# Buffers, ScalarE's order, gather pacing and one-hot layout in the expert phase of a hybrid decoder block

## The chip, the cores and the metric

The kernel runs on one core of one Trainium2 chip. The metric is the device time of one execution in microseconds (us), taken as the median of three runs. Inputs are drawn from a fixed seed, and the program is the same in every run.

## The reference, cut to what matters

A decoder layer on 512 tokens plus 16 meta tokens (width 2048): attention and an mLSTM in parallel, then a PEER layer over 16,384 experts (`u` and `v`, each 16,384 x 2048 in float32). The change touches the PEER layer alone:

```
q = (ht @ w_q)                                  # 8 heads x 2 halves x 128
s = einsum('thpd,hpnd->thpn', q, sub_keys)      # scores against 2 x 128 sub-keys
s1, i1 = top_k(s[..., 0, :], 16);  s2, i2 = top_k(s[..., 1, :], 16)
best_s, best_pos = top_k(s1[:, :, None] + s2[:, None, :], 16)
idx  = (i1 * 128 + i2) at best_pos              # 128 experts for each token
gate = softmax(best_s)
act  = gelu(einsum('td,tkd->tk', h, u[idx]))
y    = einsum('tk,tkd->td', gate * act, v[idx])
```

## The kernel before, in words

The 512 tokens are split. For 352 of them (`ND`) the kernel computes every expert densely: U multiplies them with all of `u` in 128 chunks of 128 experts, applies gelu, and stores the result in a scratch array `Ad`; a gate table `Gd`, zero except where an expert was chosen, is built beside it; V multiplies `Ad` times `Gd` with all of `v`. For the other 160 tokens the chosen rows of `u` and `v` are gathered from memory, one row for each token (128 rows of 8 KB) in one indirect DMA that GpSimd issues. There are 320 such gather steps (`NJ`): 160 with `u`, then 160 with `v`. VectorE takes each: a multiply with an accumulated sum for `u` (L844), a scaled addition for `v` (L855, L857). Three row buffers `ug` rotate.

**Chunks.** A float32 weight is split into a high and a low part, both in TensorE's faster float32 form, and each product takes three matmuls (L89 to L91): 48 for a chunk of U. `load_half` (L70) loads half a chunk, 512 KB, into a buffer `raw` by SyncE's DMA queue; `split_half` (L75) makes `hi` on ScalarE (L79, tiles `hid`, in V `hiv`) and `lo` on VectorE (L80, `lod`, `lov`). Three `raw` and five `hi` and `lo` buffers rotate; the number in a tile's name is the step, 16 more than the chunk of U. `u_chunk` (L886) runs `step`: split the next chunk, 48 matmuls into a PSUM tile `pu`, then gelu on ScalarE into `at` (L889) and its DMA to `Ad` on ScalarE's queue (L890).

**Gate table.** From chunk 33 on, each chunk of U is followed by one group of `gbuild` (five times two) until chunk 115, 88 groups in all. A group covers four tokens. `ebuild` makes, ahead of it, the one-hot rows of the two index halves for these tokens (`e`, two VectorE operations, L1076 and L1077), the second times the three bfloat16 parts of the gate (`ea` on ScalarE, L1081; `eg` on VectorE, L1079). These tiles hold the four tokens interleaved: `[128, 128, 4]`, so that one token's 128 values lie 8 bytes apart, but for `ea`, which is contiguous. `gbuild` runs 12 matmuls 128 x 128 x 128 in bfloat16 (L1092: for each token one with `ea` and two with `eg` as the moving side, `e` always as the weights) into `pg`, and ScalarE copies the group into `stg` (L1093). There is one `stg` buffer; eight groups fill it, and then SyncE's queue writes its 2 MB to `Gd` (L1095).

**Pacing.** `run(n)` takes gather steps until n are done and prefetches three. In U, `pace(c)` spreads them evenly from chunk 33 to the last one so that `JU` = 150 are done at the end of U; V takes the rest, evenly. The last six chunks of U (`UTAIL`) are also where the first eight tiles of V's moving side are prepared: `p_load` (DMAs of `gt` from `Gd`, `av` from `Ad`, on ScalarE's queue), `p_mul` (`tm`, VectorE), `p_split` (`ah` on ScalarE, `al` on VectorE). V then takes 240 half chunks of `v` through eight PSUM banks (`tmm`, L1275 to L1277: 24 matmuls each) and 16 more in another form.

**Order.** PE's program order is written by hand throughout (`manual_schedule`), VectorE's from the routing on, GpSimd's from the gate table on. ScalarE's and SyncE's orders come from a scheduler, which places an instruction by when it expects its inputs.

Of the kernel before, what the change touches and what calls it, by code (L numbers as in the profile page):

```python
# [43 lines left out]
ND = S - 128 - NB  # L44
GROUPS = [8] + [16] * 7 + [8]
NJ = 2 * (128 + SB)
JU = 150
AR = 20
AR1 = 8

# [1 line left out]
def bcast(ap, n):  # L52
    return bass.AP(tensor=ap.tensor, offset=ap.offset, ap=[list(a) for a in ap.ap] + [[0, n]])


def bcast_mid(ap, n):
    a = [list(p) for p in ap.ap]
    return bass.AP(tensor=ap.tensor, offset=ap.offset, ap=a[:1] + [[0, n]] + a[1:])


def body(tc, I, out):
    nc = tc.nc
    top = ExitStack()
    with top:
# [3 lines left out]
        dp = top.enter_context(tc.tile_pool(name="dp", bufs=1, space=DRAM))  # L68

        def load_half(src, name, rawp=None):  # L70
            raw = (rawp or wp).tile([128, 8, 128], F, name="raw" + name, tag="raw", bufs=3)
            nc.sync.dma_start(raw, src.rearrange("p (k c) -> p k c", k=8))
            return raw

        def split_half(src, name, raw=None, eng=nc.vector):  # L75
            raw = raw or load_half(src, name)
# [6 lines left out]
        def split_tile(src, name):  # L83
            return [split_half(src[b], f"{name}_{b}") for b in range(2)]

        def mm3(ps, w, k, xh, xl, cs):
            hi, lo = w[k // 8]
# [578 lines left out]
def rest(tc, I, out, L):  # L666
# [150 lines left out]
    up = sU.enter_context(tc.tile_pool(name="up", bufs=1))  # L817
    iota = up.tile([128, 128], F, name="iota")
    nc.scalar.dma_start(iota, I["c_iota"])
    iota4 = up.tile([128, 128, 4], BF, name="iota4")  # L820
    nc.vector.tensor_copy(iota4, bcast(iota, 4))
    n1T = up.tile([128, ND], BF, name="n1T")
    n2T = up.tile([128, ND], BF, name="n2T")
    gp = up.tile([128, 3, ND], BF, name="gp")
# [46 lines left out]
    sp = [I["wq"][i] for i in range(16)] + [I["u"][c] for c in range(NK)]  # L871
    w[2] = split_tile(sp[2], "d2")

    def step(n, mid=None):
        if n + 1 < len(sp):
            w[n + 1] = split_tile(sp[n + 1], f"d{n + 1}")
        ps = pmu.tile([128, 512], F, name="pu", tag="pu")
        nn = S if n < 16 else ND
        for k in range(KD):
            mm3(ps[:, :nn], w[n], k, h2h, h2l, slice(0, nn))  # L880
            if k == 7 and mid:
                mid()
# [180 lines left out]

    with tc.tile_pool(name="gk", bufs=1, reuse_waits="tile") as gk, \
            tc.tile_pool(name="psg", bufs=2, space=PSUM) as psg, \
            tc.manual_schedule(engines={mybir.EngineType.Pool}):
        stg = {}

        ge = {}

        def ebuild(q):
            t0 = 4 * q
            e = gk.tile([128, 2, 128, 4], BF, name="e", tag="e", bufs=2)
            eg = gk.tile([128, 2, 128, 4], BF, name="eg", tag="eg", bufs=2)
            ea = gk.tile([128, 4, 128], BF, name="ea", tag="ea", bufs=2)
            nc.vector.tensor_tensor(e[:, 0], iota4, bcast_mid(n1T[:, t0:t0 + 4], 128), op=OP.is_equal)  # L1076
            nc.vector.tensor_tensor(e[:, 1], iota4, bcast_mid(n2T[:, t0:t0 + 4], 128), op=OP.is_equal)  # L1077
            for i in range(2):
                nc.vector.tensor_tensor(eg[:, i], e[:, 1], bcast_mid(gp[:, 1 + i, t0:t0 + 4], 128), op=OP.mult)  # L1079
            for j in range(4):  # L1080
                nc.scalar.activation(ea[:, j, :], e[:, 1, :, j], AF.Copy, scale=g0[:, t0 + j:t0 + j + 1])  # L1081
            ge[q] = e[:, 0], [ea.rearrange("p j n -> p n j"), eg[:, 0], eg[:, 1]]

        def gbuild(q):
            tg, r = divmod(4 * q, TG)
            if r == 0:
                stg[tg] = gk.tile([128, NK, TG], F, name="stg", tag="stg")
            e1, eg = ge.pop(q)
            pg = psg.tile([128, 4, 128], F, name="pg", tag="pg")
            for j in range(4):  # L1090
                for i in range(3):
                    nc.tensor.matmul(pg[:, j, :], e1[:, :, j], eg[i][:, :, j], start=(i == 0), stop=(i == 2))  # L1092
            nc.scalar.copy(stg[tg][:, :, r:r + 4], pg.rearrange("p j n -> p n j"))  # L1093
            if r + 4 == TG:
                nc.sync.dma_start(Gd[tg, :, 0:NK, :], stg[tg])  # L1095

        gr2.append(sG.enter_context(tc.tile_pool(name="gr2", bufs=1, side="right")))
        acc["D"] = gr2[0].tile([128, D], F, name="h2nB", tag="h2nB")
        for q in range(NQ):
            nc.scalar.dma_start(acc["D"][NB * q:NB * q + NB], hB)  # L1100
        ng, n0, c0 = 0, nj[1], ci
        ebuild(0)

        def pace(c):
            run(n0 + int((c + 1 - c0) * (JU - n0) / (NK - c0)))

        for c in range(ci, NK - UTAIL):
            u_chunk(c)
            while ng < min(ND // 4, (c + 1 - ci) * (ND // 4) / (NK - 12 - ci)):
                gbuild(ng)  # L1110
                ng += 1
                if ng < ND // 4:
                    ebuild(ng)
            pace(c)
    sU.close()

    with ExitStack() as sV:
        vp = sV.enter_context(tc.tile_pool(name="vp", bufs=1, side="right", reuse_waits="tile"))
        pool_order = sV.enter_context(tc.manual_schedule(engines={mybir.EngineType.Pool}))
        g0s = [sum(GROUPS[:g]) for g in range(len(GROUPS) + 1)]  # L1120
        gts, ats, tms, A = {}, {}, {}, {}

# [35 lines left out]
        def vload(i):  # L1158
            if i < len(vord):
                g, dc, pr, c = vord[i]  # L1160
                vraw[i] = load_half(I["v"][g0s[g] // 2 + pr, dc if g == NG - 1 else 2 * dc + c], "v",
                                    None if i % 6 < 3 and i < nlast - 4 else vr[0])

        def vsplit(i):
            if i < len(vord):
# [27 lines left out]
        for c in range(NK - UTAIL, NK):  # L1193
            if c == NK - 1:
                for i in range(VLA):
                    vload(i)
                    vsplit(i)
            u_chunk(c)
            for _ in range(-(-len(pro) // (NK - c))):
                f, q = pro.pop(0)  # L1200
                f(q)
            pace(c)
        assert not pro
        sQ.close()
        sD.close()
# [258 lines left out]
```

## Time and profile before

| | |
|---|---|
| Median of three runs | 3330.11 us (3321.87 to 3330.35) |
| Profiled execution | 3331.74 us, its span 3330.0 us, mean granted clock 0.992 |
| TensorE busy | 98% of the span (20,126 matmuls) |
| VectorE, ScalarE, GpSimd busy | 70%, 40%, 28% |
| Moved by DMA | 815.47 MB, 245 GB/s over the span |

The profile follows one execution. Busy shares of TensorE count overlapping matmuls, so that the engine can be called busy while it runs slower than it could; the number of matmuls in a stretch tells more. "Idle before" is the time that an engine stood still before an instruction, with what ended it.

### The profile page before, as it was taken

How to read it: one execution, taken by the hardware profiler on the slowest of the kernel's cores; microseconds unless marked ns; L12 is line 12 of the kernel's file. 1: busy time of each engine (PE TensorE's matmuls, PEld its weight loads, DVE VectorE, ACT ScalarE, POOL GpSimd, SP SyncE). 2: the span in 40 equal slices, each digit the busy share in tenths (PEclk: the TensorE clock that was granted, in tenths of full speed). 3: DMA queues.
4: the chain of work that ended last, by engine and by line, in shares of the span. 5: the costliest groups of instructions: out<-in, count | busy, mean ns of one | idle time of the engine just before them, and what ended most of it. 6: DMA issues, size and time to landing. Idle time of an engine off the chain costs nothing.

```text
span 3330.0 us, 51020 instructions
## 1 busy us (share of the span) xinstructions
PE 3264.0 (98%) x20126; PEld 3067.1 (92%) x20126; DVE 2320.2 (70%) x3504; ACT 1325.5 (40%) x2219; POOL 943.9 (28%) x942
## 2 busy tenths in 40 slices
PE   8999999999999999999999999997999999999998
PEld 7889898888887899999999999997999999999996
DVE  7444444444367788787877778767888888888973
ACT  5444444453252233444544544433333333333323
POOL 2011111110015566423332233322323323323312
PEclk8999999999999999999999999998999999999999
DMA  4222121123353266588888978999999999999972
GB/s 154 70 70 77 64 77 64 64 70 115 127 186 136 87 221 226 206 323 316 332 343 325 361 297 348 354 362 337 377 354 375 372 365 370 375 364 372 379 279 101
DMA packets 230162, 815.47 MB, mean 245 GB/s; under 512 B 21697, under 2 KB 85697, under 8 KB 186529
## 3 DMA queue, kind: packets, MB, share of 16 engines
q1 hardware_dynamic: 105488, 400.72, 33.3%
q0 software_dynamic: 46080, 335.56, 25.7%
q10 hardware_dynamic: 78352, 75.92, 6.8%
q8 instruction: 158, 2.59, 0.3%
q14 instruction: 84, 0.68, 0.1%
HBM read 757.33 MB, written 54.79 MB: 244 GB/s over the span
## 4 chain that ended last, share of the span: by engine, by line
PE 85%; DVE 8%; DMA 2%; issue 2%; ACT 1%; POOL 1%; ACTq 0%; SPq 0%; POOLq 0%; DVEq 0%
PE pu L89 10%; PE pu L90 10%; PE pu L91 10%; PE py L1275 8%; PE py L1277 8%; PE py L1276 8%; PE ps L89 5%; PE ps L91 5%; PE ps L90 5%; PE pg L1092 3%; PE po L742 2%; PE po L740 2%; PE po L741 2%; DVE y L857 1%; DVE lov L80 1%
## 5 line engine op out<-in xcount | busy, mean ns | idle before, releaser
L89 PE MATMUL pu<-hh,hid 128*128 128x352 f32 (+1 forms) x2272 | 759.8, 334 | 0.2 <-ACT at L889 0.2
L90 PE MATMUL pu<-hh,lod 128*128 128x352 f32 (+1 forms) x2272 | 751.3, 331 | 3.1 <-DVE lod L80 3.1
L91 PE MATMUL pu<-hl,hid 128*128 128x352 f32 (+1 forms) x2272 | 750.2, 330 | 0.0
L1275 PE MATMUL py<-ah,hiv 128*128 128x352 f32 x1920 | 627.0, 327 | 20.5 <-ACT hiv L79 9.5
L1276 PE MATMUL py<-ah,lov 128*128 128x352 f32 x1920 | 623.4, 325 | 8.8 <-DVE lov L80 8.8
L1277 PE MATMUL py<-al,hiv 128*128 128x352 f32 x1920 | 625.5, 326 | 0.0
L79 ACT CAST hiv<-rawv 128x1024 fp32r<-128x1024 f32 x256 | 269.2, 1053 | 572.4 <-PE py L1277 462.6
L80 DVE TENSOR_TENSOR lod<-rawd,hid 128x1024 fp32r<-128x1024 f32 x284 | 361.0, 1287 | 176.7 <-ACT hid L79 175.5
L90 PEld LDWEIGHTS pu<-hh,lod 128*128 128x128 f32 x2272 | 428.2, 188 | 12.8 <-DVE lod L80 3.4
L89 PEld LDWEIGHTS pu<-hh,hid 128*128 128x128 f32 x2272 | 429.9, 189 | 10.3 <-ACT at L889 0.8
L91 PEld LDWEIGHTS pu<-hl,hid 128*128 128x128 f32 x2272 | 428.1, 188 | 9.7
L79 ACT CAST hid<-rawd 128x1024 fp32r<-128x1024 f32 x284 | 297.8, 1050 | 347.2 <-DMA rawd<-in_u_dram 235.1
L89 PE MATMUL ps<-xh,hiz 128*128 128x256 f32 (+2 forms) x1280 | 410.9, 321 | 1.3 <-DVE qT L369 1.2
L836 POOL DMA_INDIRECT ug<-in_un_dram,idx x128 | 249.2, 1947 | 522.3 <-DVE ug L844 500.8
L91 PE MATMUL ps<-xl,hiz 128*128 128x256 f32 (+2 forms) x1280 | 392.8, 307 | 0.0
L90 PE MATMUL ps<-xh,loz 128*128 128x256 f32 (+2 forms) x1280 | 392.5, 307 | 0.0
L1275 PEld LDWEIGHTS py<-ah,hiv 128*128 128x128 f32 x1920 | 363.0, 189 | 24.2 <-issue 12.9
L1276 PEld LDWEIGHTS py<-ah,lov 128*128 128x128 f32 x1920 | 362.6, 189 | 11.8 <-DVE lov L80 11.8
L836 POOL DMA_INDIRECT ug<-in_vn_dram,idx x128 | 229.0, 1789 | 469.7 <-DVE y L857 444.3
L1277 PEld LDWEIGHTS py<-al,hiv 128*128 128x128 f32 x1920 | 361.9, 188 | 0.0
L80 DVE TENSOR_TENSOR lov<-rawv,hiv 128x1024 fp32r<-128x1024 f32 x256 | 313.4, 1237 | 33.7 <-ACT hiv L79 33.5
L857 DVE SCALAR_TENSOR_TENSOR y<-ug,act,y 128x2048 f32<-128x2048 f32 x127 | 298.3, 2349 | 14.8 <-DMA ug<-in_vn_dram,idx 14.8
(342 smaller groups left out, 5029.9 us busy)
## 6 DMA issues: line engine op xcount, KB each, us to landing
rawd<-in_u_dram SPq DMA_DIRECT2D x256, 512.0 KB
rawv<-in_v_dram SPq DMA_DIRECT2D x256, 512.0 KB
rawz<-in_wz_dram SPq DMA_DIRECT2D x98, 512.0 KB
Ad<-at ACTq DMA_DIRECT2D x128, 176.0 KB
Gd<-stg SPq DMA_DIRECT2D x11, 2048.0 KB
gt<-Gd ACTq DMA_DIRECT2D x32, 704.0 KB
av<-Ad ACTq DMA_DIRECT2D x64, 352.0 KB
rawwo<-in_wo_dram SPq DMA_DIRECT2D x40, 512.0 KB
```

Of the source, the lines that this page charges most:

```text
L79: nc.scalar.copy(hi, raw)
L80: eng.tensor_tensor(lo, raw, hi.bitcast(F), op=OP.subtract)
L89: nc.tensor.matmul(ps, a, xh[k][:, cs], start=(k == 0), stop=False)
L90: nc.tensor.matmul(ps, b, xh[k][:, cs], start=False, stop=False)
L91: nc.tensor.matmul(ps, a, xl[k][:, cs], start=False, stop=(k == KD - 1))
L740: nc.tensor.matmul(ps[tb], mh[n][:, sl], h, start=(n == 0), stop=False)
L836: nc.gpsimd.indirect_dma_start(out=t, out_offset=None, in_=I["un" if kind in "dD" else "vn"], in_offset=bass.IndirectOffsetOnAxis(ap=ix[:, ...
L857: nc.vector.scalar_tensor_tensor(acc[kind], t, o, acc[kind], op0=OP.mult, op1=OP.add)
L1092: nc.tensor.matmul(pg[:, j, :], e1[:, :, j], eg[i][:, :, j], start=(i == 0), stop=(i == 2))
L1275: nc.tensor.matmul(po, h, ah, start=(pr + j == 0), stop=False)
L1276: nc.tensor.matmul(po, l, ah, start=False, stop=False)
L1277: nc.tensor.matmul(po, h, al, start=False, stop=(2 * pr + j == n - 1))
```

## The change

Five `raw` buffers stand in U from the gate table on: the three of before and two in a pool of their own, taken in turn. The split of a chunk is issued two chunks ahead, right behind the store of `at`, where it was one chunk ahead. ScalarE's order is written by hand from the gate table on (through the rest of U, and V). `JU` is 166, and the gather steps are paced to end at chunk 121, so that the last six chunks hold none; V is left with 154 where it had 170. The one-hot tiles hold two tokens interleaved, twice (`[128, 2, 128, 2]`), so that a token's values lie 4 bytes apart.

```diff
-JU = 150
+JU = 166
-            raw = (rawp or wp).tile([128, 8, 128], F, name="raw" + name, tag="raw", bufs=3)
+            pool, n = rawp or (wp, 3)
+            raw = pool.tile([128, 8, 128], F, name="raw" + name, tag="raw", bufs=n)
...
-    iota4 = up.tile([128, 128, 4], BF, name="iota4")
-    nc.vector.tensor_copy(iota4, bcast(iota, 4))
+    iota2 = up.tile([128, 2, 128, 2], BF, name="iota2")
+    for i in range(2):
+        nc.vector.tensor_copy(iota2[:, i], bcast(iota, 2))
...
+    ru = []
+
+    def uload(n):
+        if n < len(sp) and n not in w:
+            ps = [None, None]
+            if ru:
+                for b in range(2):
+                    if ru[1] % 5 in (1, 3):
+                        ps[b] = (ru[0], 2)
+                    ru[1] += 1
+            w[n] = split_tile(sp[n], f"d{n}", ps)
+
     def step(n, mid=None):
-        if n + 1 < len(sp):
-            w[n + 1] = split_tile(sp[n + 1], f"d{n + 1}")
+        uload(n + 1)
...
         nc.scalar.dma_start(Ad[c // 4, :, c % 4, :], at)
+        if ru:
+            uload(c + 18)
...
-            tc.manual_schedule(engines={mybir.EngineType.Pool}):
+            tc.manual_schedule(engines={mybir.EngineType.Pool, mybir.EngineType.Activation}), \
+            tc.tile_pool(name="ru", bufs=1, reuse_waits="tile") as rup:
         stg = {}
+        ru += [rup, 0]
+
+        def pairs(t):
+            a = [list(p) for p in t.ap]
+            return bass.AP(tensor=t.tensor, offset=t.offset, ap=[a[0], [2 * a[1][0], 2], [0, 128], [a[1][0], 2]])
...
-            nc.vector.tensor_tensor(e[:, 0], iota4, bcast_mid(n1T[:, t0:t0 + 4], 128), op=OP.is_equal)
+            nc.vector.tensor_tensor(e[:, 0], iota2, pairs(n1T[:, t0:t0 + 4]), op=OP.is_equal)
...
-                    nc.tensor.matmul(pg[:, j, :], e1[:, :, j], eg[i][:, :, j], start=(i == 0), stop=(i == 2))
+                    nc.tensor.matmul(pg[:, j, :], e1[:, j // 2, :, j % 2], eg[i][:, j // 2, :, j % 2],
+                                     start=(i == 0), stop=(i == 2))
...
-            run(n0 + int((c + 1 - c0) * (JU - n0) / (NK - c0)))
+            run(n0 + int((c + 1 - c0) * (JU - n0) / (NK - UTAIL - c0)))
...
+        ru.clear()
...
-        pool_order = sV.enter_context(tc.manual_schedule(engines={mybir.EngineType.Pool}))
+        pool_order = sV.enter_context(tc.manual_schedule(engines={mybir.EngineType.Pool, mybir.EngineType.Activation}))
...
                 f(q)
-            pace(c)
```

PE's order is the same instruction for instruction. ScalarE's around chunk 79 of U (step 95), where a new `stg` begins, stood so before:

```order
L1081 ACTIVATE ea_18178<-e_18176,g0_9082 128x128 x4
L79 CAST hid95_1_18198<-rawd95_1_18196 128x1024
L889 ACTIVATE at_18158<-pu_18109 128x352
L890 DMA Ad_9071<-at_18158 128x352
L1081 ACTIVATE ea_18270<-e_18268,g0_9082 128x128 x4
L1093 COPY stg_18161<-pg_18162 128x128x4
L79 CAST hid96_0_18287<-rawd96_0_18285 128x1024
L79 CAST hid96_1_18293<-rawd96_1_18291 128x1024
```

And so it stands now, at the same place:

```order
L1116 COPY stg_17527<-pg_18117 128x128x4
L1102 ACTIVATE ea_18134<-e_18132,g0_9083 128x128 x4
L902 ACTIVATE at_18198<-pu_18149 128x352
L903 DMA Ad_9071<-at_18198 128x352
L80 CAST hid95_0_18203<-rawd95_0_18201 128x1024
L80 CAST hid95_1_18209<-rawd95_1_18207 128x1024
L1116 COPY stg_18213<-pg_18214 128x128x4
L1102 ACTIVATE ea_18230<-e_18228,g0_9083 128x128 x4
```

Where a new `stg` begins (`stg_18161`, now `stg_18213`), its first copy stood behind the `ea` of the next group; now it stands ahead of it. Both halves of `hid` for a step stand together, behind `at` and its store.

VectorE's order around step 141 (chunk 125, one of the last six) stood so before (`ug` with `actB` is a gather step):

```order
L844 SCALAR_TENSOR_TENSOR ug_22097,actB_9063<-ug_22097,h2nB_13800 128x2048
L844 SCALAR_TENSOR_TENSOR ug_22164,actB_9063<-ug_22164,h2nB_13800 128x2048
L80 TENSOR_TENSOR lod141_0_22339<-rawd141_0_22336,hid141_0_22338 128x1024
L80 TENSOR_TENSOR lod141_1_22345<-rawd141_1_22342,hid141_1_22344 128x1024
L1146 TENSOR_TENSOR al_22401<-tm_22328,ah_22400 128x352
L1135 TENSOR_TENSOR tm_22404<-av_22243,gt_22239 128x352
L1146 TENSOR_TENSOR al_22407<-tm_22404,ah_22406 128x352
L844 SCALAR_TENSOR_TENSOR ug_22248,actB_9063<-ug_22248,h2nB_13800 128x2048
```

Now the same stretch of VectorE reads:

```order
L1170 TENSOR_TENSOR al_22402<-tm_22399,ah_22401 128x352
L1159 TENSOR_TENSOR tm_22409<-av_22327,gt_22323 128x352
L81 TENSOR_TENSOR lod141_0_22414<-rawd141_0_22411,hid141_0_22413 128x1024
L81 TENSOR_TENSOR lod141_1_22420<-rawd141_1_22417,hid141_1_22419 128x1024
L1170 TENSOR_TENSOR al_22476<-tm_22409,ah_22475 128x352
L1159 TENSOR_TENSOR tm_22479<-av_22327,gt_22323 128x352
L1170 TENSOR_TENSOR al_22482<-tm_22479,ah_22481 128x352
L81 TENSOR_TENSOR lod142_0_22490<-rawd142_0_22487,hid142_0_22489 128x1024
```

The gather steps are gone from it; the splits and the preparation of V's first tiles stay.

## Rows read from the trace of the kernel before

**Rows 1.** The page: busy us of each engine; shares of the last chain.

```profile
PE 3264.0 (98%) x20126; PEld 3067.1 (92%) x20126; DVE 2320.2 (70%) x3504; ACT 1325.5 (40%) x2219; POOL 943.9 (28%) x942
PE 85%; DVE 8%; DMA 2%; issue 2%; ACT 1%; POOL 1%; ACTq 0%; SPq 0%; POOLq 0%; DVEq 0%
```

**Rows 2.** Stretches: U with gate groups, its end, V's start, V.

```profile
core 0: us, PE busy (x) PEld busy (x) DVE busy (x) ACT busy (x) POOL busy (x), PEclk, DMA share, GB/s
1411.00:2164.00 753.00, 752.43 (x5099) 740.25 (x5098) 591.28 (x762) 368.02 (x701) 235.12 (x118) 1.00 0.87 332
2164.00:2264.00 100.00, 94.74 (x578) 93.63 (x576) 64.34 (x69) 31.82 (x44) 28.15 (x15) 0.98 0.94 357
2264.00:2380.00 116.00, 99.93 (x564) 96.65 (x565) 84.39 (x96) 42.10 (x67) 32.22 (x19) 0.93 0.94 351
2380.00:3190.00 810.00, 798.72 (x4914) 795.58 (x4914) 710.21 (x655) 259.45 (x303) 265.05 (x148) 1.00 0.97 368
```

**Rows 3.** Tile pg, 1440 to 2160: matmul durations in ns, min/median/max.

```profile
L1092 PE MATMUL pg<-eg,e x671: 273/294/303, 1439.7 to 2155.0; 128*128 128x128 bf16 x168
L1092 PE MATMUL pg<-ea,e x335: 237/238/249, 1439.9 to 2154.8; 128*128 128x128 bf16 x168
```

**Rows 4.** Timeline of PE around one gate group: start us, us, what.

```profile
1707.13 0.32 PE L90 MATMUL pu<-hh,lod 128*128 128x352 f32 x1
1707.29 0.32 PE L91 MATMUL pu<-hl,hid 128*128 128x352 f32 x1
...
1708.81 0.32 PE L90 MATMUL pu<-hh,lod 128*128 128x352 f32 x1
```

**Rows 5.** VectorE by group, 1440 to 2160: busy us, mean ns.

```profile
L844 DVE SCALAR_TENSOR_TENSOR ug<-ug,h2n 128x2048 f32<-128x2048 f32 x109 | 246.9, 2286 | 1.3 <-DMA ug<-in_un_dram,idx 1.3
L80 DVE TENSOR_TENSOR lod<-rawd,hid 128x1024 fp32r<-128x1024 f32 x163 | 196.4, 1222 | 89.2 <-ACT hid L79 88.5 <-issue 0.7
L1079 DVE TENSOR_TENSOR eg<-e,gp 128x512 bf16<-128x512 bf16 x166 | 63.2, 422 | 2.8
```

**Rows 6.** GpSimd's DMA queue, 1440 to 2160: packets, MB, share of 16 engines.

```profile
q0 software_dynamic: 16449, 119.82, 43.5%
```

**Rows 7.** DMA rate in 40 equal slices of 2160 to 2380.

```profile
GB/s 407 394 415 412 341 316 415 413 246 417 408 350 193 311 403 394 199 395 382 372 395 415 156 116 380 407 366 399 339 359 364 396 349 335 328 374 381 378 380 373
```

**Rows 8.** ScalarE's waits, 1410 to 2170: us in total, times, longest.

```profile
ACT stg L1093 <- DMA Gd<-stg: 32.0, 9, 6.2
```

**Rows 9.** SyncE's and ScalarE's timelines: three of ten stores of `stg`, next copy.

```profile
1477.20 0.33 SPq L1095 DMA_DIRECT2D Gd<-stg  x1
1490.70 0.59 ACT L1093 COPY stg<-pg 128x512 f32<-128x512 f32 x1 [4.05 <-DMA Gd<-stg]
...
1548.29 0.33 SPq L1095 DMA_DIRECT2D Gd<-stg  x1
1548.36 1.32 ACT L1081 ACTIVATE ea<-e,g 128x128 bf16<-128x128 bf16 x4
...
1564.22 0.59 ACT L1093 COPY stg<-pg 128x512 f32<-128x512 f32 x1 [6.20 <-DMA Gd<-stg]
...
2094.16 0.33 SPq L1095 DMA_DIRECT2D Gd<-stg  x1
2104.56 0.59 ACT L1093 COPY stg<-pg 128x512 f32<-128x512 f32 x1 [1.25 <-DMA Gd<-stg]
```

**Rows 10.** PE's timeline at the end of U and in V's start.

```profile
2252.65 0.48 PE L90 MATMUL pu<-hh,lod 128*128 128x352 f32 x1 [3.11 <-DVE lod L80]
...
2283.10 0.66 PE L1275 MATMUL py<-ah,hiv 128*128 128x352 f32 x1 [7.18 <-ACT hiv L79]
```

**Rows 11.** ScalarE's timeline in V's start.

```profile
2264.03 4.85 ACTq L890 DMA_DIRECT2D Ad<-at  x1
...
2282.00 1.05 ACT L79 CAST hiv<-rawv 128x1024 fp32r<-128x1024 f32 x1 [10.03 <-DMA rawv<-in_v_dram]
```

**Rows 12.** PE's waits in V, 2400 to 3190: us in total, times, longest.

```profile
PE py L1275 <- DVE yT L1287: 8.9, 10, 1.0
```

More of the change, by code (lines that the diff above doesn't have):

```diff
@@ L70, in load_half, with split_half @@
         def load_half(src, name, rawp=None):
-            raw = (rawp or wp).tile([128, 8, 128], F, name="raw" + name, tag="raw", bufs=3)
+            pool, n = rawp or (wp, 3)
+            raw = pool.tile([128, 8, 128], F, name="raw" + name, tag="raw", bufs=n)
             nc.sync.dma_start(raw, src.rearrange("p (k c) -> p k c", k=8))
             return raw
-        def split_half(src, name, raw=None, eng=nc.vector):
-            raw = raw or load_half(src, name)
+        def split_half(src, name, raw=None, eng=nc.vector, rawp=None):
+            raw = raw or load_half(src, name, rawp)
             hi = wp.tile([128, 8, 128], R, name="hi" + name, tag="whi")
@@ L81, in split_half, with split_tile @@
             return hi, lo
-        def split_tile(src, name):
-            return [split_half(src[b], f"{name}_{b}") for b in range(2)]
+        def split_tile(src, name, rawps=(None, None)):
+            return [split_half(src[b], f"{name}_{b}", rawp=rawps[b]) for b in range(2)]
         def mm3(ps, w, k, xh, xl, cs):
@@ L1065, in rest @@
             tc.tile_pool(name="psg", bufs=2, space=PSUM) as psg, \
-            tc.manual_schedule(engines={mybir.EngineType.Pool}):
+            tc.manual_schedule(engines={mybir.EngineType.Pool, mybir.EngineType.Activation}), \
+            tc.tile_pool(name="ru", bufs=1, reuse_waits="tile") as rup:
         stg = {}
+        ru += [rup, 0]
         ge = {}
+        def pairs(t):
+            a = [list(p) for p in t.ap]
+            return bass.AP(tensor=t.tensor, offset=t.offset, ap=[a[0], [2 * a[1][0], 2], [0, 128], [a[1][0], 2]])
         def ebuild(q):
             t0 = 4 * q
-            e = gk.tile([128, 2, 128, 4], BF, name="e", tag="e", bufs=2)
-            eg = gk.tile([128, 2, 128, 4], BF, name="eg", tag="eg", bufs=2)
-            ea = gk.tile([128, 4, 128], BF, name="ea", tag="ea", bufs=2)
-            nc.vector.tensor_tensor(e[:, 0], iota4, bcast_mid(n1T[:, t0:t0 + 4], 128), op=OP.is_equal)
-            nc.vector.tensor_tensor(e[:, 1], iota4, bcast_mid(n2T[:, t0:t0 + 4], 128), op=OP.is_equal)
+            e = gk.tile([128, 2, 2, 128, 2], BF, name="e", tag="e", bufs=2)
+            eg = gk.tile([128, 2, 2, 128, 2], BF, name="eg", tag="eg", bufs=2)
+            ea = gk.tile([128, 2, 2, 128], BF, name="ea", tag="ea", bufs=2)
+            nc.vector.tensor_tensor(e[:, 0], iota2, pairs(n1T[:, t0:t0 + 4]), op=OP.is_equal)
+            nc.vector.tensor_tensor(e[:, 1], iota2, pairs(n2T[:, t0:t0 + 4]), op=OP.is_equal)
             for i in range(2):
-                nc.vector.tensor_tensor(eg[:, i], e[:, 1], bcast_mid(gp[:, 1 + i, t0:t0 + 4], 128), op=OP.mult)
+                nc.vector.tensor_tensor(eg[:, i], e[:, 1], pairs(gp[:, 1 + i, t0:t0 + 4]), op=OP.mult)
             for j in range(4):
-                nc.scalar.activation(ea[:, j, :], e[:, 1, :, j], AF.Copy, scale=g0[:, t0 + j:t0 + j + 1])
-            ge[q] = e[:, 0], [ea.rearrange("p j n -> p n j"), eg[:, 0], eg[:, 1]]
+                nc.scalar.activation(ea[:, j // 2, j % 2, :], e[:, 1, j // 2, :, j % 2], AF.Copy,
+                                     scale=g0[:, t0 + j:t0 + j + 1])
+            ge[q] = e[:, 0], [ea.rearrange("p a b n -> p a n b"), eg[:, 0], eg[:, 1]]
         def gbuild(q):
@@ L1161, in vload @@
                 vraw[i] = load_half(I["v"][g0s[g] // 2 + pr, dc if g == NG - 1 else 2 * dc + c], "v",
-                                    None if i % 6 < 3 and i < nlast - 4 else vr[0])
+                                    None if i % 6 < 3 and i < nlast - 4 else (vr[0], 3))
         def vsplit(i):
```

## Prediction

> **What bounds the kernel now.** I read the page first: TensorE is busy for 98% of the span and holds 85% of the chain that ended last, VectorE 8% [rows 1]. So the time is TensorE's work, its pace, and the holes in it. The table of stretches tells where the holes are [rows 2]. In the 753 us of U that hold gate groups TensorE has no hole, at a granted clock of 1.00, and the timeline gives its pace: one matmul of 352 columns every 0.16 us (1707.13 to 1707.29) [rows 4]. At that pace the 100 us at U's end would hold 625 matmuls; they hold 578, so 47 x 0.16 = 7.5 us are lost. V does 4914 in 810 us, 6.07 a us; the 116 us of V's start hold 564 where 704 would fit: 140 / 6.07 = 23.1 us lost, at a granted clock of 0.93 (part of the stretch at the 1.2 GHz level, after TensorE had stood still). Together 30.6 us. The timelines name the cause, late loads: 3.11 us for a low part, 7.18 us for a high part of `v` [rows 10], whose load ScalarE itself awaited for 10.03 us; the last store to `Ad` took 4.85 us to issue into full queues [rows 11]. In V the waits of TensorE are short ones on VectorE's additions into `yT`, 8.9 us in ten [rows 12].
>
> **One-hots in pairs.** The price of a gate group: from the last matmul before it to the second after it pass 1.52 us, where two steps would be 0.32 [rows 4]; so 1.20 us a group, 88 groups, 106 us, all on TensorE. Twelve matmuls share it. The eight whose moving side has its values 8 bytes apart take 294 ns, the four with a contiguous one 238 [rows 3]; the shape is the same. If 4 bytes are as good as contiguous, 8 x 56 = 0.45 us of each group goes, 39 us in all. That 4 bytes a column keep pace is shown by the float32 matmuls: 352 columns of 4 bytes in 160 ns, 0.45 ns a column. At that pace 12 x 58 ns = 0.70 us, the most that can go is 0.50 x 88 = 44 us. The least is nothing. I take 0.38 us a group, near the 0.45 and not at it because the weights are strided too and each matmul loads its own: **-33 us**.
>
> The Trainium skill, page "SBUF — State Buffer", section "Door 1: The DMA port swizzle", says that two accesses to a 16-byte line already give full bandwidth; 8 bytes apart is two to a line, and the pairs would bring nothing. The 56 ns between the two kinds speak against it [rows 3]. The page "TensorE: Matmul & The Clock Gate" of the same skill, section "Back-to-back issue gap", gives about 81 ns a matmul for 128 columns when each loads weights: a group would be 0.97 us, and the term 20 us, not 33.
>
> VectorE's four one-hot operations keep their count and size, 422 ns each [rows 5]. I cost them at nothing. Should the third dimension slow them to the pace of the float32 split (1222 ns for 1024, so 0.61), a chunk gains some 0.8 us of VectorE.
>
> **Sixteen more gather steps in U, in fewer chunks.** The first gather steps (15) precede the gate groups. The paces are (150-15)/95 = 1.42 a chunk before and (166-15)/89 = 1.70 now. VectorE: 591 us in 83 chunks is 7.1 us each [rows 2]; 0.28 x 2.29 us more [rows 5] makes 7.8 in a chunk of (753-33)/83 = 8.7 us. It is hidden, by 0.9 us; that is also what covers slower one-hots. DMA: 332 GB/s x 753 us / 83 is 3.01 MB a chunk; 0.28 rows of 1.05 MB make it 3.30, 381 GB/s. The share of 0.87 at 332 would be full at 382; slices at U's end reach 417 [rows 7]; V held 368 at 0.97 [rows 2]. I take no loss; at V's rate a chunk would last 8.97 us, 25 us more in all. Five buffers make a late load harmless: a load may now start five halves ahead, not three.
>
> **ScalarE by hand: a wait that takes another's place.** Each eighth group ends a `stg`, whose store must land before the next copy. The scheduler had put that copy behind the next `ea`; now `ea` stands behind it, and the next group of TensorE behind `ea`. ScalarE waited there before, 32.0 us in nine waits [rows 8], at no cost to TensorE. Behind it now stand `ea`, `at`, its store and two `hid`. Price: gelu, two `hid` of 1.05 us [rows 11] and the copy of 0.59 put the store's issue some 3.3 us behind a chunk's end. The next copy but one chunk later may start L after that, L being the time to landing: 13.5 us for the first of ten, 10.4 for the last, 15.9 for the longest, 12.2 on average [rows 9]. Then 0.59 of copy and 1.32 of four `ea`. TensorE wants them two chunks of 8.50 us (8.88 less 0.38) after the first chunk's end, the last of the four tokens 0.6 later. It waits 3.3 + L + 1.9 - 17.6 = L - 12.4. With the old ten L the positive parts sum to 9 us. But GpSimd's queue held 43.5% of the DMA engines [rows 6]; with 1.70/1.42 of the rows in 8.50/8.88 of the time it holds 54%, and what is left for the store falls from 56.5% to 45.5%: L is 1.24 times as long, the sum 30 us. Between the two I take **+17 us**. Elsewhere in U the fixed order asks for `hid` at the chunk's end and leaves 8.5 us; free.
>
> **The last six chunks, and V's start.** 1.42 x 6 = 8.5 gather steps leave them, 8.9 of the 36 MB that the stretch moved, and 19 us of VectorE's 64. Loads, stores and V's first loads then meet emptier queues. What stays: the handover of the PSUM banks, and `gt` and `av`, which ScalarE now issues only behind chunk 122, with `tm` ahead of a `lod` on VectorE. All 30.6 us can come back, or, if V's fourth load still waits for the last store, about 12. I take **-26**, near the whole, since each wait there ended on a DMA.
>
> **V.** It has 16 steps fewer: 16 x 2.29 = 37 us less of VectorE, 17 MB less in 810 us at a DMA share of 0.97. Only the waits on `yT` can gain, and a little pace: 0 to 12 us. ScalarE's new order follows VectorE's here, both ahead of TensorE; nothing. I take **-3**.
>
> **Sum.** -33 + 17 - 26 - 3 = -45. The profiled execution took 3331.7 us (span 3330.0), 1.6 above the median of the runs: 3286.7, so 3285 beside the median. The ends: 44 + 0 + 30.6 + 12 makes -87; 0 + 30 - 12 + 25 makes +43.
>
> **Rivals.**
> - The store of `stg` stays short. For it: six of the ten L were under 12.4, and no hole in TensorE. Pairs 40, U's end 29, V 5, waits 1: 73 less, **3257**.
> - DMA is the bound in U. For it: 381 GB/s asked, 368 held in V. Against: slices of 417. -33 + 25 + 17 - 24 - 3 = -18: **3312**.
> - The pairs change nothing (the SBUF rule above). Against it: 56 ns. A chunk stays at 8.88, waits begin at an L of 13.2, 8 us in all: 8 - 26 - 3 = -21, **3309**.
> - Slower: the copy behind the store. Without that wait the change is worth 62 us, so ten waits of over 6.2 us eat it, from an L of 18.6 on. At an L of 21 us (2.6 MB, the store and a half chunk ahead of it, at 125 GB/s) ten waits of 8.6 make 86 us: **3354**. For it: the order is fixed, and 15.9 was seen. Against: the mean of 12.2 would have to grow by more than half.
>
> **Chances.** Forecast 0.50 (its own range 3270 to 3298), short stores 0.18, DMA bound 0.15, no gain from pairs 0.10, slower 0.07. The range goes from 3252 to 3314 and leaves out the slower case and the far ends of the others. Within 0.3% (10 us, about what a measurement of this kernel tells from no change) lies only the tail of the two cases near 3310: 0.05. Faster 0.88, slower 0.07.
>
> **What would show it.** The pairs: `eg` matmuls near 238 ns, a group near 0.82 us. The store: in the list of waits TensorE's `pg` on ScalarE's `ea`, up to ten times, 1 to 4 us each. U's end: no wait of TensorE over 3 us from chunk 116 to V's fourth half chunk, and a granted clock of 1.00 there. V: the DMA share under 0.97. The forecast is wrong if U shows waits on `lod` or `hid` (DMA), if `eg` stays near 294 ns, or if `pg` waits over 6 us a time.

## The result, and the profile after

The changed kernel takes 3363.09 us (median, 3360.15 to 3367.12), the kernel before 3330.12 us beside it: a ratio of 1.0105, 95% interval 1.009 to 1.012. It is slower by 33 us; 3285 us and a range of 3252 to 3314 were forecast, and a chance of 0.07 for slower. The profiled execution took 3361.8 us, its span 3360.0.

The first view is the page: busy us of each engine, and the shares of the chain that ended last. They answer to [rows 1].

```profile
PE 3245.4 (97%) x20122; PEld 3051.2 (91%) x20126; DVE 2322.1 (69%) x3505; ACT 1313.6 (39%) x2219; POOL 887.2 (26%) x942
PE 81%; DVE 7%; DMA 5%; issue 3%; ACT 2%; POOL 1%; ACTq 1%; SPq 0%; DVEq 0%; POOLq 0%
```

TensorE still holds the chain, but for 81% where it held 85%: it stands still more often. Where, say the same four stretches as in [rows 2], with the same columns.

```profile
1411.00:2164.00 753.00, 704.89 (x4872) 692.89 (x4871) 606.15 (x768) 347.95 (x669) 211.82 (x132) 0.96 0.89 344
2164.00:2264.00 100.00, 93.78 (x605) 92.96 (x604) 74.28 (x73) 35.09 (x55) 30.29 (x19) 0.98 0.99 382
2264.00:2380.00 116.00, 105.33 (x624) 103.59 (x624) 80.00 (x84) 46.13 (x74) 19.29 (x13) 0.96 0.89 315
2380.00:3190.00 810.00, 793.14 (x4848) 789.06 (x4848) 672.48 (x631) 252.05 (x303) 234.77 (x133) 0.99 0.92 347
```

The gate-group part of U, which had no hole at a clock of 1.00, now issues 227 matmuls fewer in the same time (4872, 5099 before), at 0.96. Since U lasts longer, the later windows no longer hold the same work, so I cut the trace at events instead: first and last `pg` matmul, last `pu` matmul, end of TensorE's work.

| us | before | after |
|---|---|---|
| up to the first gate group | 1419.5 | 1416.8 |
| U with gate groups | 744.6 | 775.7 |
| U's end | 97.9 | 101.4 |
| V to TensorE's last matmul | 1055.7 | 1054.0 |
| of that, V's first 704 matmuls | 141.2 | 128.7 |
| of that, the rest of V | 914.5 | 925.3 |
| to the end | 12.2 | 12.2 |

U with gate groups loses 31.1 us, about as much as the whole kernel. V as a whole looks unchanged, but hides a gain of 12.5 us in its first 704 matmuls (as many as V's pace would fit into the 116 us of V's start in [rows 2]) and a loss of 10.8 behind them. The list of TensorE's waits names the places (us in total, times, longest). The first two lines are the stretch with gate groups, where before no wait was over 0.3 us; the `yT` lines are V's and the last is U's end.

```profile
PE pg L1114 <- ACT ea L1102: 28.5, 7, 5.0
PE pg L1114 <- DVE eg L1100: 19.6, 4, 5.2
PE py L1298 <- DVE yT L1310: 14.8, 9, 3.5
PE py L1298 <- ACT yT L1308: 9.1, 2, 4.8
...
PE pu L91 <- DVE lod L81: 6.2, 1, 6.2
```

The seven waits of the first line are the store waits that were forecast. Here is the first of them on ScalarE (start us, us, what, idle before), and TensorE's gate group behind it:

```profile
1484.69 2.00 ACT L80 CAST hid<-rawd 128x1024 fp32r<-128x1024 f32 x2 [0.40 <-ACT at L902]
1496.27 0.59 ACT L1116 COPY stg<-pg 128x512 f32<-128x512 f32 x1 [9.58 <-DMA Gd<-stg]
1496.75 1.28 ACT L1102 ACTIVATE ea<-e,g 128x128 bf16<-128x128 bf16 x4
```
```profile
1497.20 0.27 PE L1114 MATMUL pg<-ea,e 128*128 128x128 bf16 x1 [4.99 <-ACT ea L1102]
...
1497.80 0.31 PE L1114 MATMUL pg<-ea,e 128*128 128x128 bf16 x1
```

ScalarE stands 9.58 us at the copy, `ea` comes behind it, and TensorE loses 4.99 us; then its matmuls run at the lower of its two clock levels, 1.2 GHz: the granted clock is 0.50 from 1495 to 1501.5 us, and a matmul takes 0.31 us where 0.22 is usual.

The four waits of the second line are new. They lie in the chunks that hold two gate groups, between the first and the second. The timeline of all engines around 1616:

```profile
1615.76 0.47 ACT L902 ACTIVATE at<-pu 128x352 f32<-128x352 f32 x1 [2.13 <-PE pu L92]
...
1616.15 0.28 PE L1114 MATMUL pg<-eg,e 128*128 128x128 bf16 x2
...
1616.62 1.99 ACT L80 CAST hid<-rawd 128x1024 fp32r<-128x1024 f32 x2 [0.40 <-ACT at L902]
...
1617.70 2.36 DVE L81 TENSOR_TENSOR lod<-rawd,hid 128x1024 fp32r<-128x1024 f32 x2 [0.17 <-ACT hid L80]
1618.52 0.58 ACT L1116 COPY stg<-pg 128x512 f32<-128x512 f32 x1
...
1619.98 0.42 DVE L1097 TENSOR_TENSOR e<-iota,n1T 128x512 bf16<-128x512 bf16 x1
1620.32 0.42 DVE L1098 TENSOR_TENSOR e<-iota,n2T 128x512 bf16<-128x512 bf16 x1
...
1620.77 1.28 ACT L1102 ACTIVATE ea<-e,g 128x128 bf16<-128x128 bf16 x4 [1.67 <-DVE e L1098]
...
1621.22 0.26 PE L1114 MATMUL pg<-ea,e 128*128 128x128 bf16 x1 [4.79 <-DVE eg L1100]
```

To read it, follow the starts downward: end of the chunk, `at`, two `hid`, two `lod`, `e`, `ea` and `eg`, gate group. Each waits for the one above, on its own engine or on the other: 5.5 us from 1615.76 to 1621.22. In them TensorE ends the first group, at 1616.43, and then stands still for 4.79 us.

The sum for this stretch, from TensorE's starts: 88 groups of 1.07 us and not 1.52 give back 39.3; the store holes cost 29.7, other holes before `pu` 3.0, the double groups 19.4 more than before, matmuls at the lower clock 16.6, the rest 1.8. That is +31.2; measured are +31.1.

The pairs did more than forecast. Tile `pg`, with the columns of [rows 3]:

```profile
L1114 PE MATMUL pg<-eg,e x704: 218/218/314, 1416.8 to 2192.2; 128*128 128x128 bf16 x176
L1114 PE MATMUL pg<-ea,e x352: 216/218/312, 1416.8 to 2192.1; 128*128 128x128 bf16 x176
```

### The profile page after: what moved, and what is told of

The parts are those of the page before. It is cut to its first block, busy times and chain, and to the rows that moved or that the text cites. A ratio compares the mean times of both kernels' runs of the same rounds, so it can differ in the third digit from the quotient of the medians.

```text
span 3360.0 us, 51062 instructions
## 1 busy us (share of the span) xinstructions
PE 3245.4 (97%) x20122; PEld 3051.2 (91%) x20126; DVE 2322.1 (69%) x3505; ACT 1313.6 (39%) x2219; POOL 887.2 (26%) x942
## 4 chain that ended last, share of the span: by engine, by line
PE 81%; DVE 7%; DMA 5%; issue 3%; ACT 2%; POOL 1%; ACTq 1%; SPq 0%; DVEq 0%; POOLq 0%
PE pu L90 9%; PE pu L91 9%; PE pu L92 9%; PE py L1298 7%; PE py L1300 7%; PE py L1299 7%; PE ps L90 5%; PE ps L92 5%; PE ps L91 5%; DMA Gd<-stg 3%; PE po L743 2%; PE po L741 2%; PE po L742 2%; PE pg L1114 2%; DVE lov L81 1%
## 5 line engine op out<-in xcount | busy, mean ns | idle before, releaser
L80 ACT CAST hiv<-rawv 128x1024 fp32r<-128x1024 f32 x256 | 260.0, 1047 | 270.9 <-PE py L1300 165.2
L838 POOL DMA_INDIRECT ug<-in_un_dram,idx x128 | 204.6, 1599 | 495.2 <-DVE ug L846 473.4
L80 ACT CAST hid<-rawd 128x1024 fp32r<-128x1024 f32 x284 | 288.0, 1047 | 120.1 <-PE pu L92 52.0
L846 DVE SCALAR_TENSOR_TENSOR ug<-ug,h2n 128x2048 f32<-128x2048 f32 x128 | 289.8, 2285 | 20.2 <-DMA ug<-in_un_dram,idx 20.2
```

The lines of the kernel that those rows point to most:

```text
L838: nc.gpsimd.indirect_dma_start(out=t, out_offset=None, in_=I["un" if kind in "dD" else "vn"], in_offset=bass.IndirectOffsetOnAxis(ap=ix[:, ...
L846: nc.vector.scalar_tensor_tensor(t, t, 1.0, acc[kind], op0=OP.mult, op1=OP.mult, accum_out=o)
```

## The experiments

All times are medians of four runs (ten in experiment 4); the kernel before ran beside them each time, at 3326 to 3329 us. Stretches are cut as in the table above; V runs to TensorE's last matmul.

**1. ScalarE given back to the scheduler.**

```diff
-            tc.manual_schedule(engines={mybir.EngineType.Pool, mybir.EngineType.Activation}), \
+            tc.manual_schedule(engines={mybir.EngineType.Pool}), \
...
-        pool_order = sV.enter_context(tc.manual_schedule(engines={mybir.EngineType.Pool, mybir.EngineType.Activation}))
+        pool_order = sV.enter_context(tc.manual_schedule(engines={mybir.EngineType.Pool}))
```

> The changed kernel with ScalarE's order given back to the scheduler, in U and in V; pairs, gather pace and five raw buffers stay. In the order that comes out the next gate group's ea stands ahead of the stg copy again (a lead of 0.9 groups on average, as before the change, where the changed kernel has none). Theory A (the lead was what TensorE lived on; writing ScalarE's order by hand took it away): the seven holes behind a Gd store (29.7 us) and the four where two groups follow each other (20.5 us) go, and with them 12 us of slow clock; the wait on lod at U's end (6.4) and the two on yT copies at V's start (9.4) may go too. 3363 - 62 = 3301, down to 3285 with the last two. Theory B (the DMA engines: 1.70 gather steps a chunk make the stores late, L 14.9 instead of 12.2): the stores stay as late and TensorE still waits in U, above 3340. Theory C (VectorE's two early lod of a chunk stand ahead of the one-hots, from the five raw buffers): the four double groups keep their 5 us, the seven store holes go: near 3320.

Measured 3271.32 (ratio to before 0.983, 0.9813 to 0.9846). U with gate groups 715.6, U's end 95.6, V 1028.2. Theory A's side, below its range. The seven store holes are gone; of the four between double groups two are left, the whole of TensorE's `pg` waits in this stretch:

```profile
PE pg L1114 <- DVE eg L1100: 7.1, 2, 4.3
```

So the rest of the change gains 57 us, and the hand order costs 92: 60 in U with gate groups, 6 at U's end, 26 in V.

**2. One-hots ahead of the copy, by hand.** The next group's `ebuild` goes inside `gbuild`, between the matmuls and the copy.

```diff
+            if q + 1 < ND // 4:
+                ebuild(q + 1)
             nc.scalar.copy(stg[tg][:, :, r:r + 4], pg.rearrange("p j n -> p n j"))
...
-                if ng < ND // 4:
-                    ebuild(ng)
```

> The changed kernel with one thing moved: the next group's one-hots (ebuild) are issued ahead of the stg copy of the present group, not behind it. ScalarE stays in program order, everything else stays. Theory A (lead of one group): 11 holes of U go, 50 us, and 12 us of slow clock: 3301, U's stretch with gate groups some 715 us instead of 775.7; the holes at U's end and in V stay. Theory B (DMA): Gd's L stays near 15 and the wait only moves to at or hid: 3340 or more. Theory C (VectorE's lod ahead of e): the store holes go, the double groups still wait: near 3325.

Measured 3354.27 (1.0081, 1.0065 to 1.0098): only 9 us of the 62. Theory A as I put it falls. TensorE's waits in the stretch, and ScalarE and VectorE in one of them:

```profile
PE pg L1114 <- DVE eg L1100: 41.1, 12, 5.1
```
```profile
1496.06 0.59 ACT L1118 COPY stg<-pg 128x512 f32<-128x512 f32 x1 [7.21 <-DMA Gd<-stg]
1496.54 0.47 ACT L902 ACTIVATE at<-pu 128x352 f32<-128x352 f32 x1
...
1497.41 2.00 ACT L80 CAST hid<-rawd 128x1024 fp32r<-128x1024 f32 x2 [0.40 <-ACT at L902]
1498.49 2.36 DVE L81 TENSOR_TENSOR lod<-rawd,hid 128x1024 fp32r<-128x1024 f32 x2 [5.74 <-ACT hid L80]
1500.77 0.42 DVE L1097 TENSOR_TENSOR e<-iota,n1T 128x512 bf16<-128x512 bf16 x1
1501.10 0.42 DVE L1098 TENSOR_TENSOR e<-iota,n2T 128x512 bf16<-128x512 bf16 x1
1501.55 0.98 ACT L1102 ACTIVATE ea<-e,g 128x128 bf16<-128x128 bf16 x3 [2.15 <-DVE e L1098]
```

`ea` stands ahead of its copy, but what it reads does not: the previous copy holds `hid`, and through `lod` on VectorE it holds `e`. A lead counted on one engine is none while the other engine follows.

**3. The pairs alone**, put into the kernel before.

> The kernel before with the pairs alone. The changed kernel's group took 1.07 us from the last matmul before it to the second after it, where it was 1.52: 0.447 x 88 = 39 us. All theories: 3330 - 39 = 3291, if no wait takes its place. Were the pairs themselves to bring waits (chunks shorter by 0.45 us, so that loads and stores come late by as much), 3300 to 3315.

Measured 3305.34 (0.9934, 0.9917 to 0.995), 14 us above 3291. U with gate groups falls by 31.0 (713.6) and not 39: waits of TensorE there, 5.7 us in six, 3.5 of them on `at`, take some of it. U's end grows from 97.9 to 106.4, with 6.0 us of waits on `at`. That loads and stores have less time in the shorter chunks would explain both; no run tries it.

**4. Pairs and the gather pace**, three raw buffers, ScalarE free.

> The kernel before with the pairs and the gather pace of the change (166 steps in U, none in its last six chunks); three raw buffers, ScalarE by the scheduler. Theory A: the pace costs nothing in U (the lead of one group covers a longer L) and gives back part of the 30.6 us at U's end: 3291 less 10 to 26, so 3265 to 3281. Theory B (1.70 steps a chunk overload the DMA engines): U loses 20 us or more to loads and stores, so 3295 to 3315, and Gd's L rises to 15 here too.

Measured 3323.88 (0.9989, 0.9978 to 1.0001). U with gate groups grows from 713.6 to 760.3, V falls from 1053.2 to 1024.8. ScalarE's and TensorE's waits in U's stretch:

```profile
ACT hid L79 <- DMA rawd<-in_u_dram: 308.8, 140, 6.2
ACT stg L1100 <- DMA Gd<-stg: 56.5, 10, 7.2
```
```profile
PE pu L89 <- ACT at L890: 18.8, 9, 5.1
PE pg L1098 <- ACT ea L1086: 9.3, 4, 6.6
```

With three buffers ScalarE waits for a load 140 times, `at` behind it holds a PSUM bank of U, and TensorE stands. With five buffers and the split two chunks ahead (experiment 1) ScalarE's wait on `rawd` is 7.0 us in all; no run has one of these two without the other. This is Theory B's side, above its range; but L, the time from a store's issue to the next copy, is 13.0 us on average here and not 15 (12.6 in experiment 3), so the store is the smaller part (the 9.3 us on `ea`).

**5. One-hots first, the early split last.** As in 2, and `uload(c + 18)` moved behind the groups.

```diff
-        if ru:
-            uload(c + 18)
...
                 ng += 1
+            uload(c + 18)
             pace(c)
```

> The changed kernel, ScalarE still in program order in U and V, with two things moved: the next group's one-hots ahead of the present group's stg copy, and the split of the half chunks two ahead (hid, lod) behind both, where the changed kernel has it ahead of them. Theory D (what TensorE lost in U is a chain in fixed order: chunk end, at, two hid, two lod on VectorE, e, ea; 5.0 us long, as the 5.0 us between two groups of one chunk show; a store wait on ScalarE is added to it): the one-hots now wait for nothing but at and free buffers, so the store holes go, the holes of double groups shrink from 5.0 to some 1.3 us, and the slow clock behind them goes. U's stretch with gate groups falls from 775.7 to some 718; with U's end and V as they were 3305. Theory E (any order by hand stalls ScalarE in U, since it then stands at a late load or store and all else stands behind it): the wait only moves again, as it did when the one-hots alone were moved (3354): 3335 or more.

Measured 3426.91 (1.03, 1.0283 to 1.0317), worse by 64 us than the changed kernel. U with gate groups takes 831.5. Theory D in this form is refuted. VectorE's and ScalarE's longest waits:

```profile
DVE lod L81 <- ACT hid L80: 207.2, 84, 8.1
```
```profile
ACT ea L1100 <- DVE e L1096: 345.6, 70, 6.2
```

The two engines wait for each other in every chunk: `e`, `ea`, copy, `hid`, `lod`, gathers, the next `e`. A chunk is 831.5/83 = 10.0 us: 7.5 of VectorE's work (450.6 busy of the 600 us from 1500 on) and 2.5 of its wait for `hid`. That loop, not TensorE, set the pace; I had looked at TensorE's side only.

**6. The same with ScalarE free in V.**

> The same two moves, and ScalarE's order left to the scheduler in V; in U it stays by hand. Theory D: V's 1053 us become the 1028 of the kernel with a free ScalarE, and U is as in the run with the two moves alone: 3305 less 26, and less some 6 at U's end: 3273 to 3279. Theory E: above 3305.

Measured 3391.99 (1.0191, 1.0174 to 1.0208). U is as bad as in 5 (831.7); V falls from 1057.0 to 1031.3. V's part of the expectation held (26 us), U's not.

**7. ScalarE free in U, by hand in V.**

> The changed kernel with ScalarE by the scheduler in U's stretch alone; in V and the last six chunks it stays in program order. If the losses in the two parts are independent (60 us in U's stretch, 32 in U's end and V, together the 92 between 3363 and 3271): 3271 + 32 = 3303. If V's loss comes only from what U left late (stores, gathers): near 3275.

Measured 3310.39 (0.9942, 0.9921 to 0.9963): U with gate groups 720.6, V 1059.5. So the hand order costs 53 us in U and 39 in V and U's end (35 between experiments 5 and 6).

**8. The changed kernel with the old gather pace.**

> The changed kernel with the gather pace of before (150 steps in U, spread to the last chunk); ScalarE by hand, pairs and five raw buffers stay. Theory D: the four holes of 5.0 us between double groups stay, since no gather is in that chain; Gd's L falls from 14.9 to some 12.5, so the store holes fall by some 15 to 20 us with their slow clock; U's end gets its gathers back: 3335 to 3355. Theory B (the DMA engines are what makes U late): all eleven holes go: 3300 to 3315.

Measured 3387.78 (1.0178, 1.0161 to 1.0195), a miss upward: V takes 1095.5, 41.5 us more, with 16 gather steps more there; with ScalarE free the same steps cost V 27 (experiments 12 and 1). In U it answers the question: the stretch with gate groups falls by 11 us only, to 764.5. Its waits:

```profile
PE pg L1114 <- ACT ea L1102: 19.7, 6, 5.2
PE pg L1114 <- DVE eg L1100: 19.4, 4, 5.0
```

With fewer gathers the four holes of double groups are unchanged and the store holes only somewhat smaller. Theory B falls for the changed kernel.

**9. One-hots two groups ahead, ScalarE by hand throughout.**

```diff
         ebuild(0)
+        ebuild(1)
...
                 gbuild(ng)
                 ng += 1
-                if ng < ND // 4:
-                    ebuild(ng)
+                if ng + 1 < ND // 4:
+                    ebuild(ng + 1)
```

> The changed kernel, ScalarE by hand throughout, with the one-hots built two groups ahead: a group's ea and e are issued behind the copy of the group two before it, where the changed kernel has them behind the copy of the group just before it. Their two buffers each suffice. Theory F (in program order a group's one-hots lie in the same chunk as the group before it, behind that chunk's at, hid, lod; the 5.0 us holes of the double groups are that chain, and a store wait is added to it; one whole chunk of lead takes both out): the eleven holes and their slow clock go, U's stretch from 775.7 to 720 or less, the rest stays: 3363 - 53 = 3310, as with ScalarE free in U alone. Theory G (VectorE has no time left in U, 484 busy and 117 in waits of 600 us, so that any order in which ScalarE gives it hid only behind at is late): the holes move to lod, hid or at, 3345 or more.

Measured 3298.12 (0.9906, 0.9889 to 0.9922), 65 us less than the changed kernel by four lines. U with gate groups is 712.6. Theory F holds, G falls; of the eleven holes one is left, between two groups of one chunk. ScalarE at the same store and TensorE's waits in the stretch:

```profile
1488.62 0.59 ACT L1116 COPY stg<-pg 128x512 f32<-128x512 f32 x1 [9.33 <-DMA Gd<-stg]
```
```profile
PE pg L1114 <- DVE eg L1100: 3.1, 1, 3.1
PE pu L91 <- DVE lod L81: 1.9, 3, 0.8
```

ScalarE waits for the store as long as before (9.33 us, 9.58 in the changed kernel), and TensorE notices nothing: what it needs next was built a chunk earlier.

**10. The same, and half chunks split three ahead** (`uload(c + 19)`).

> The same, and the half chunks split three ahead instead of two (behind a chunk's at the split for the chunk three later), as the scheduler's order has it. Theory F: the one-hots were what was missing: as the run with the one-hots two ahead alone, 3310 give or take 8. Theory G: this gives VectorE its hid a chunk earlier; 3310 only here, and the one-hots alone stay above 3345.

Measured 3305.58 (0.9929, 0.9912 to 0.9945): within Theory F's range, though 7 us above experiment 9; U with gate groups 716.9. The split needed no more lead.

**11. In V, `ah` one half chunk later**, with ScalarE free in U.

```diff
                 for f, q in prep.get(i, ()):
-                    f(q)
+                    if f is p_split:
+                        late.append(q)
+                    else:
+                        f(q)
...  in the next step, behind vsplit and yadd:
+            while late:
+                p_split(late.pop(0))
```

> ScalarE by the scheduler in U and by hand in V (3310), with one thing moved in V: each ah (and al) is issued one half chunk later than its tm, behind the next half chunk's hiv. Theory H (in V ScalarE by hand stands at ah until VectorE has made tm, which is itself behind a gather; hiv stands behind it, lov behind hiv, and the additions to yT behind lov): the waits of TensorE on yT, 14.8 us, go, and with them slow clock: 3310 - 20 = 3290, to 3280. Rival (what costs V is ScalarE's own DMA issues into full queues, 3 us each, with the yT copies behind): 3305 or more.

Measured 3268.74 (0.9817, 0.9801 to 0.9833), 42 less than experiment 7 and more than expected: V falls from 1059.5 to 1022.9. TensorE's wait on `yT` in 2300 to 3200, in 7 and here:

```profile
PE py L1298 <- DVE yT L1310: 15.4, 9, 3.6
```
```profile
PE py L1298 <- DVE yT L1310: 0.3, 1, 0.3
```

The place of `ah` is the cause, as Theory H has it. What it does there is less sure: the rival's wait, on the `yT` copies behind ScalarE's DMA issues, goes as well (4.7 to 0.6 us). No issue was moved, but those on ScalarE's queue that took over 1 us fell from 23, 57.3 us in all, to 5 with 12.6 (both from 2300 to 3200). The run does not separate the wait at `ah` from the long issues that come with it.

**12. The old pace with ScalarE free and five buffers.**

> Pairs and five raw buffers, ScalarE by the scheduler, and the gather pace of before (150 steps in U, spread to the last chunk). It prices the pace with five raw buffers. If V's 25 us come from its 16 gather steps fewer (1052 us with pairs alone, 1028 with the new pace): V is 1052 again and U's stretch 713 as it was: 3271 + 24 = 3295, some 5 more at U's end: 3300. If the five raw buffers or the free ScalarE made V faster: 3275.

Measured 3296.09 (0.9902, 0.9885 to 0.9918): V 1055.4, U with gate groups 710.8. The pace is worth 25 us, nearly all in V, once five buffers carry it in U.

**13. By hand throughout, both moves (9 and 11).**

> The changed kernel, ScalarE by hand in U and V, with both moves: one-hots two groups ahead in U, and in V each ah a half chunk later, behind the next hiv. If the two places are the whole loss and independent: 3298 (one-hots alone) - 42 (the V move, 3310 to 3269) = 3256, within 8; below the 3271 of the kernel whose ScalarE is left free. If hand order costs something of its own beside these places: 3275 or more.

Measured 3270.28, 3261.85 to 3274.89 (0.9824, 0.98 to 0.9848). My sum was wrong: the move in V is worth 28 us here, not 42, since V in 9 had 1051.9, not the 1059.5 of 7, and could fall to 1022.9 by 29 only, to 3269. That is as fast as with ScalarE free; the hand order itself costs nothing that these runs show.

**14. And the first `tm` of V one chunk later.**

```diff
-            for _ in range(-(-len(pro) // (NK - c))):
+            for _ in range(4 if c == NK - UTAIL else -(-len(pro) // (NK - c))):
```

> The same, and the first tm of V is issued one chunk later, so that on VectorE it stands behind the two lod of chunk 124 and not ahead of them. In the run with the one-hots two ahead, tm waited there 12.0 us for its load from Ad, and TensorE 9.1 for lod. If that order makes the hole at U's end: it goes, 6 to 9 us with some slow clock, 3248. If the load queue is what is late (lod's own half chunk not landed either): no change, 3256.

Measured 3266.81, 3254.25 to 3273.12 (0.9826, 0.9806 to 0.9846). The times do not separate it from 13. The traces do at the place itself, TensorE's waits at U's end in 13 and in 14:

```profile
PE pu L91 <- DVE lod L81: 7.4, 1, 7.4
```
```profile
PE pu L91 <- DVE lod L81: 0.8, 1, 0.8
```

The hole is gone, and U's end takes 93.9 and not 102.9. Experiments 1, 11, 13 and 14 are all faster than both kernels, and not told apart.

## Why the prediction was wrong, step by step

The forecast was a sum of four terms: pairs -33, the store wait +17, U's end and V's start -26, V -3. Without the second, -62 in all for what is not ScalarE's order. Experiment 1 measures that rest: 3328.07 to 3271.32, -57. So the failed step is the second, "ScalarE by hand: a wait that takes another's place": +17 was written where 92 stand, 60 of them in U with gate groups, 6 at U's end and 26 in V. That the other three came to nearly their sum is partly luck: in experiment 1 U with gate groups falls by 29.0 us (pairs, -33), U's end and V's first 704 matmuls by 16.3 (-26), the rest of V by 13.5 (-3). Two errors of 10 us cancel.

- **The store wait itself** was the right mechanism. It was priced L - 12.4, up to 30 us; seven holes make 29.7, the upper bound; the formula, with the ten L measured, gives 29.1. L averages 14.9 us in the changed kernel (from a store's issue to the next copy), against 15.1 at the upper bound and 12.2 before. But the reason for the longer L, the gathers' share of the DMA engines, is only part: with ScalarE free and the same gathers it is 12.6, by hand with the old pace 13.8; what else makes it longer stays open. And L decides nothing by itself: with the one-hots two ahead it is 15.5 and TensorE does not wait.
- **"Elsewhere in U the fixed order asks for `hid` at the chunk's end and leaves 8.5 us; free"** was false. I had priced one group a chunk. The 88 groups lie in 84 chunks, four of which hold two (not five, as the description of the kernel has it); there the chain of 5.5 us has no chunk to lie in. It was put at nothing and cost 19.4 us.
- **The lower clock behind the holes**, 16.6 us, was in no term. Each hole is charged twice: by its length and by the slower matmuls behind it.
- **U's end and V's start**: -26 expected; -9.0 came, +3.5 at U's end and -12.5 in V's first 704 matmuls. The prediction had named the cause at U's end among what stays ("`tm` ahead of a `lod` on VectorE"), gave it no price, and took nearly the whole. VectorE stood 7.34 us for `av`, and two `lod` behind it:

```profile
2258.63 0.52 DVE L1159 TENSOR_TENSOR tm<-av,gt 128x352 f32<-128x352 f32 x1 [7.34 <-DMA av<-Ad]
2259.07 2.35 DVE L81 TENSOR_TENSOR lod<-rawd,hid 128x1024 fp32r<-128x1024 f32 x2
```

- **V**: two errors that nearly cancel. The gather pace was worth 27 us in V (1055.4 to 1028.2, experiments 12 and 1): 14 in the first 704 matmuls, which the term above covers, and 13 in the rest, four times the -3 and just over its bound of 12. "ScalarE's new order follows VectorE's here, both ahead of TensorE; nothing" was false: in the rest of V the hand order costs 24 us (925.3, and 901.0 in experiment 1). By hand ScalarE stands at `ah` until `tm` is made. ScalarE's waits from 2300 to 3200 in the changed kernel, and in experiment 1:

```profile
ACT ah L1169 <- DVE tm L1159: 348.7, 106, 9.3
ACT hiv L80 <- PE py L1300: 135.7, 48, 3.3
```
```profile
ACT hiv L80 <- PE py L1300: 451.9, 201, 3.2
ACT ah L1169 <- DVE tm L1159: 87.8, 70, 2.7
```

  Left free, ScalarE waits for TensorE to release a buffer, that is, it is ahead; by hand it waits for VectorE, and `hiv`, `lov` and the additions to `yT` come late. Moving `ah` alone takes the loss away (experiment 11).
- **The pairs**: right, and mis-sized by the room around them. A group fell by 0.45 us and not 0.38, 39 us; alone they gave 23 (experiment 3). The Trainium skill, page "SBUF — State Buffer", section "Door 1: The DMA port swizzle", says that two accesses to a 16-byte line are enough for full bandwidth, by which 8 bytes apart would lose nothing; 294 ns at 8 bytes and 218 at 4 say otherwise here. The 81 ns a matmul of the Trainium skill's page "TensorE: Matmul & The Clock Gate", section "Back-to-back issue gap", is undercut too: the median step from one start to the next within a group is 58 ns, where it was 98.
- **Five raw buffers and DMA in U**: right in the main. No loss to the DMA engines was taken, and with ScalarE free the new pace costs U with gate groups 5 us (710.8 and 715.6, experiments 12 and 1). The worth of the buffers, with the split two ahead, was in the interaction: the new pace costs 19 us with three (3 to 4) and gains 25 with five (12 to 1); at the old pace they give 9 (3 to 12).

Of the rivals, the slower one gave 3354, near the 3363 measured, but by 86 us of store waits where there are 29.7; its number was right by accident. Of what was to show the steps, V's DMA share of 0.92 came out, and the signs of the pairs and the store went further than asked: `eg` at 218 ns (238 asked) and seven waits of 3 to 5 us on `ea` (1 to 4). The wait of TensorE at U's end was 6.2 us where under 3 was asked. None of the three signs of a wrong forecast appeared in U with gate groups: no wait on `lod` or `hid`, `eg` not at 294 ns, no `pg` wait over 5.2 us. They watched the terms that had a price, and most of the error was in what had none.

## What to carry to other kernels

When an engine is put in program order, its price is not the one wait that comes to mind: for each consumer, write down the whole chain of instructions across the engines from its latest input, and ask what happens where two iterations fall together. The cure here was neither to give the order back nor to swap neighbours (one swap gained 9 us, another lost 64), but to issue a consumer's input one iteration earlier (65 us) and an instruction that waits one iteration later (42 us with ScalarE free in U, 28 by hand throughout). An engine may stand long at no cost if what lies behind it has a full iteration in hand: the same wait of 9 us at the store cost TensorE 5 us, and then none.

## What was not expected of the hardware

- The matmuls whose moving side was contiguous all along (`ea`) also went from 238 to 218 ns, and the weight loads from 117 to 102 ns (VectorE's four operations stayed at 420, as costed). Of the operands of these matmuls only the weights changed their spacing, from 8 to 4 bytes; the `eg` matmuls between them changed too, so that the weights' part is not shown by itself. These are the weight loads from 1440 to 2160, before and after (busy us, mean ns, then idle before):

```profile
L1092 PEld LDWEIGHTS <-e 128*128 128x128 bf16 x1003 | 90.4, 117 | 11.0
```
```profile
L1114 PEld LDWEIGHTS <-e 128*128 128x128 bf16 x972 | 61.2, 102 | 54.4 <-issue 31.4 <-DVE e L1097 12.6
```

- The time from a store's issue to the next copy moved with the order of other engines at least as much as with the gather pace: with ScalarE free 10.6 us at the old pace and 12.6 at the new, by hand 13.8 and 14.9, and by hand in the slower U of experiment 5 12.5. Why the order makes it longer or shorter was not tried; that two `hid` in a row release two raw buffers, and so two loads, just ahead of the store is a guess.
